# Seven block products for eight in the up projections of four feed-forwards

## The chip, the cores and the metric

The kernel runs on one core of one Trainium2 chip. The metric is the device time of one execution in microseconds (us): 3358.54 us, the median of three runs (3357.44 to 3358.71).

TensorE (PE in the profile) multiplies matrices, VectorE (DVE), ScalarE (ACT) and GpSimd (POOL) do elementwise work, and SyncE (SP) issues the transfers of the weights. PEld is TensorE's loading of the next 128x128 block of weights, beside its matmuls.

## The reference

Two blocks of two layers each, on 512 tokens of width 1024. Block 1 (with 16 meta tokens ahead, 528 in all) has a hybrid mixer and a feed-forward with a convolution. Block 2 has in each layer a feed-forward, then attention (layer 0) or a gated MLP (layer 1), then a second feed-forward. What the change touches is the four feed-forwards of block 2:

```python
def _swiglu_ffn(x, w_gate_up, w_down):
    g, u = jnp.split(x @ w_gate_up, 2, axis=-1)
    return (jax.nn.silu(g) * u) @ w_down

    for i in range(DEPTH):
        x = x + 0.5 * _swiglu_ffn(_rmsnorm(x, ffn1_norm[i]), ffn1_w_gate_up[i], ffn1_w_down[i])
        h = _rmsnorm(x, mix_norm[i])
        ...
        x = x + 0.5 * _swiglu_ffn(_rmsnorm(x, ffn2_norm[i]), ffn2_w_gate_up[i], ffn2_w_down[i])
```

Here x is 512 x 1024, w_gate_up 1024 x 5632 (2816 gates, 2816 values), w_down 2816 x 1024, all in 32-bit floats.

## The kernel before

Features lie on partitions and tokens in columns: h[0..7] are eight tiles of 128 features x 512 tokens (528 in block 1). A product is done in 128x128 blocks of weights ("slabs"). To keep 32-bit precision, weights and operands are each split into a high and a low part of 12 bits, and a slab takes three matmuls: high x high, low operand x high weight, high operand x low weight (`unit`, L204).

The weights come as units of 128 x 1024 (eight slabs, 512 KB). `WStream` (L85) holds all units in the order of their use: SP loads up to three units ahead into `wraw`, ScalarE rounds a half unit (128x512) to the high part `whi` (L124), and VectorE subtracts it from the raw weights to give the low part `wlo` (L125). Four halves of each are held. Every half unit goes through both engines once and is then used by 12 matmuls for each part of the tokens.

In block 2 a matmul has all 512 tokens as columns. In block 1 the 528 tokens (516 in its last up projections) are done in two parts of 264 (258), each with its own weight load.

A feed-forward of block 2 (`ffn2`, L534) has 22 tiles of gates and 22 of values, a unit each. `ffn_seq` (L349) goes through them in three groups, and puts the down products of a group behind the second tile of the next. For each tile VectorE multiplies the two sums by 1/rms (`yg`, `yv`), ScalarE applies silu, VectorE multiplies, and the product is split into `ghi` (ScalarE) and `glo` (VectorE). The down products of a group add into h, a tile of 128 features at a time. When a tile of h is final, `prep` (L273) makes the operands `xhi`, `xlo` of what comes next and adds its squares to `ssq`; `finish_norm` makes 1/rms of it later, beside the first unit, since it scales the result and not the operand.

The tile framework's scheduler sets the order on each engine from the order of the code and its own costs; each engine then works in that order. Sums lie in PSUM: tiles `g` and `s`, four of 512 columns each.

Of the kernel before, what the change touches and what calls it, by code (L numbers as in the profile page):

```python
# [21 lines left out]
# tokens that the last convolution of block 1 reads, in two even parts  # L22
# [7 lines left out]
FGROUPS = ((0, 6), (6, 14), (14, 22))  # L30
LEVELS = (1, 2, 4, 8, 16, 32, 64)
# [7 lines left out]
# w_in column tiles of block 1 in the order they are worked on  # L39
# [45 lines left out]
class WStream:  # L85
    """Weight units in the order of their use: loaded ahead, then split exactly into two parts of 12 bits, by halves."""

    RAW = 3
    SPLIT = 4
    HALF = 4 * P  # L90

    def __init__(self, nc, pool):
        self.nc, self.pool = nc, pool
        self.items, self.halves = [], []
        self.raw, self.sp = {}, {}
        self.n_dma = self.n_split = self.i = 0

    def add(self, key, ap):
        n = ap.shape[1]
        for a in range(0, n, self.HALF):  # L100
            self.halves.append((len(self.items), a, min(n, a + self.HALF)))
        self.items.append((key, ap, len(self.halves)))

    def _dma(self, upto):
        while self.n_dma < min(upto, len(self.items)):
            ap = self.items[self.n_dma][1]
            t = self.pool.tile([P, 2 * self.HALF], F32, tag="raw", name="wraw", bufs=self.RAW)
            n = ap.shape[1]
            for a, b in ((0, n),) if self.n_dma else ((0, self.HALF), (self.HALF, n)):
                self.nc.sync.dma_start(t[:, a:b], ap[:, a:b])  # L110
            self.raw[self.n_dma] = t
            self.n_dma += 1

    def prime(self, n):
        self._dma(n)

    def _split(self, upto):
        while self.n_split < min(upto, len(self.halves)):
            u, a, b = self.halves[self.n_split]
            self._dma(u + self.RAW)  # L120
            t, n = self.raw[u], b - a
            hi = self.pool.tile([P, self.HALF], F32R, tag="hi", name="whi", bufs=self.SPLIT)
            lo = self.pool.tile([P, self.HALF], F32R, tag="lo", name="wlo", bufs=self.SPLIT)
            self.nc.scalar.activation(out=hi[:, 0:n], in_=t[:, a:b], func=AF.Copy)  # L124
            self.nc.vector.tensor_tensor(lo[:, 0:n], t[:, a:b], hi[:, 0:n].bitcast(F32), ALU.subtract)  # L125
            self.sp[self.n_split] = (hi, lo, n // P)
            self.n_split += 1

    def prepare(self, n):
        self._split(n)  # L130

    def get(self, key):
        """the parts (hi, lo, slabs) of the next unit, one after the other"""
        u = self.halves[self.i][0]
        k, _, end = self.items[u]
        assert k == key, (k, key)
        while self.i < end:
            i = self.i
            self.i += 1
            self._split(i + self.SPLIT - 1)  # L140
            yield self.sp.pop(i)


class Model:
    def __init__(self, tc, io):
        assert set(self.MERGE) == set(range(KD))
        self.tc, self.nc, self.io = tc, tc.nc, io
        self.pending_norm = None
        self.later = []
        self.slabwise = False  # L150
        self.budget = 0.0
        self.table, self.table_load, self.table_users = None, None, []

# [18 lines left out]
    def after(self, later, earlier):  # L172
        """issue order on one engine"""
# [4 lines left out]
    def act(self, out, a, f, **k):  # L178
        """activations keep to the order of their tables, so that a table is loaded once for all that use it in a row"""
# [14 lines left out]
    def split_scaled(self, src, gcol, hi, lo):  # L194
        """hi + lo = src * gcol"""
# [8 lines left out]
    def unit(self, key, x, new=None, ps=None, first=True, final=True):  # L204
        """psum of w^T x over the slabs of a unit, in three passes"""
# [3 lines left out]
        k, last = 0, self.ws.items[self.ws.halves[self.ws.i][0]][1].shape[1] // P - 1  # L209
# [26 lines left out]
    def new_g2(self):  # L236
        """a unit of block 1 in two tiles of the other kind, for when they have nothing else to do"""
        return self.new_s(), self.new_s()

    def new_s(self):  # L240
        return self.psum.tile([P, 512], F32, tag="s", name="s", bufs=4)

    def hv(self, k):
        """the tokens that the present block works on"""
# [24 lines left out]

    def xg(self, k):  # L270
# [25 lines left out]
    def means(self, parts, ones, src):  # L296
        """means over partitions, of both parts that src is split into"""
# [1161 lines left out]
```

## Time and profile before

| | |
|---|---|
| median of three runs | 3358.54 us |
| profiled execution, first to last instruction (its span) | 3354.3 us |
| PE busy | 3335.8 us (99%), 19462 matmuls |
| PEld busy | 2894.8 us (86%) |
| DVE busy | 1891.4 us (56%) |
| ACT busy | 1440.1 us (43%) |
| DMA | 298 MB, 89 GB/s on average |

The time of the profiled execution is known only by its span, which is 4.2 us under the median of the runs. The rows of a matmul's busy time overlap each other, so the pace of TensorE is read from how many matmuls a stretch holds, not from how long one takes. The first weights of block 2's four feed-forwards are loaded at 1310, 1953, 2308 and 2961 us; attention lies between the first two feed-forwards, the gated MLP between the last two.

### The profile page before, as it was taken

The page shows a single profiled execution, that of the slowest core. Times are in us where ns is not written, and L with a number is a line of the kernel's source. Part 1 is how long each engine was busy: PE and PEld are TensorE (multiplying, and loading weights), DVE is VectorE, ACT ScalarE, POOL GpSimd, SP SyncE. Part 2 cuts the span into 40 slices and gives each one's busy share as a digit, 9 for nine tenths or more (in the row PEclk, how much of TensorE's full clock was granted, in tenths as well). Part 3 has the DMA queues.
Part 4 walks back from the last instruction along what each step waited for, and adds up shares of the span by engine and source line. Part 5 has one row for each costly group of instructions (what it writes and reads, how often), then busy time and mean ns, then how long its engine had stood idle before and what let it go on. Part 6 is the DMA issues. An engine that isn't in the chain of part 4 may idle for free.

```text
span 3354.3 us, 48141 instructions
## 1 busy us (share of the span) xinstructions
PE 3335.8 (99%) x19462; PEld 2894.8 (86%) x19462; DVE 1891.4 (56%) x3412; ACT 1440.1 (43%) x2531; POOL 15.8 (0%) x41
## 2 busy tenths in 40 slices
PE   8999999999999999999999999999999999999999
PEld 8999999999999998888887778888888888888887
DVE  7766665667665756544446764445444546554443
ACT  5664343456643435332346642324332335343322
POOL 1000000000000000000000000000000000000000
PEclk9999999999999999999999999999999999999999
DMA  3122322322223233233322123333233332223332
GB/s 127 58 64 89 90 93 89 94 76 64 70 89 95 89 95 95 87 102 94 95 88 67 45 85 94 95 95 94 90 100 94 96 118 88 88 89 94 96 96 91
DMA packets 85647, 298.24 MB, mean 89 GB/s; under 512 B 9761, under 2 KB 9761, under 8 KB 85297
## 3 DMA queue, kind: packets, MB, share of 16 engines
q1 hardware_dynamic: 83664, 289.51, 28.0%
q8 instruction: 153, 2.51, 0.3%
q0 software_dynamic: 1328, 3.56, 0.3%
q10 hardware_dynamic: 432, 2.10, 0.2%
q14 instruction: 70, 0.57, 0.1%
HBM read 293.03 MB, written 2.10 MB: 88 GB/s over the span
## 4 chain that ended last, share of the span: by engine, by line
PE 97%; ACT 1%; DVE 1%; DMA 0%; issue 0%; SPq 0%; ACTq 0%
PE g L192 89%; PE s L192 8%; DMA wraw<-w_in 0%; PE s L1182 0%; PE s L1149 0%; ACT L182 0%; DVE am L1169 0%; ACT p L186 0%; PE s L772 0%; PE s L1215 0%; ACT whi L124 0%; DVE wlo L125 0%; PE s L831 0%; ACT rtmp L186 0%; DVE s L161 0%
## 5 line engine op out<-in xcount | busy, mean ns | idle before, releaser
L124 ACT ACTIVATE whi<-wraw 128x512 fp32r<-128x512 f32 x1112 | 691.6, 623 | 1533.8 <-PE g L192 1460.3
L125 DVE TENSOR_TENSOR wlo<-wraw,whi 128x512 fp32r<-128x512 f32 x1112 | 749.2, 675 | 545.6 <-ACT whi L124 523.4
L192 PE MATMUL g<-xhi,whi 128*128 128x512 f32 (+2 forms) x3696 | 1052.6, 332 | 1.0 <-ACT whi L124 1.0
L192 PE MATMUL g<-xlo,whi 128*128 128x512 f32 (+2 forms) x3696 | 1047.1, 331 | 0.0
L192 PE MATMUL g<-xhi,wlo 128*128 128x512 f32 (+2 forms) x3696 | 1046.3, 331 | 0.2 <-DVE wlo L125 0.2
L192 PEld LDWEIGHTS g<-xhi,whi 128*128 128x128 f32 x3696 | 627.0, 189 | 72.6 <-ACT whi L124 1.2
L192 PEld LDWEIGHTS g<-xhi,wlo 128*128 128x128 f32 x3696 | 626.7, 189 | 65.9 <-DVE wlo L125 0.6
L192 PEld LDWEIGHTS g<-xlo,whi 128*128 128x128 f32 x3696 | 624.3, 189 | 66.7
L192 PE MATMUL g<-glo,whi 128*128 128x512 f32 (+1 forms) x1360 | 469.7, 366 | 0.1
L192 PE MATMUL g<-ghi,whi 128*128 128x512 f32 (+1 forms) x1360 | 469.8, 367 | 0.0
L192 PE MATMUL g<-ghi,wlo 128*128 128x512 f32 (+1 forms) x1360 | 469.7, 367 | 0.0
L192 PEld LDWEIGHTS g<-glo,whi 128*128 128x128 f32 x1360 | 244.0, 188 | 45.8 <-DVE glo L161 0.5
L192 PEld LDWEIGHTS g<-ghi,whi 128*128 128x128 f32 x1360 | 244.0, 188 | 45.3 <-ACT ghi L186 0.2
L192 PEld LDWEIGHTS g<-ghi,wlo 128*128 128x128 f32 x1360 | 243.8, 188 | 45.5
L161 DVE TENSOR_TENSOR yv<-g,rstd 128x512 f32<-128x512 f32 x88 | 60.9, 692 | 132.7 <-PE g L192 132.7
L170 DVE SCALAR_TENSOR_TENSOR h<-g,h 128x512 f32<-128x512 f32 x96 | 66.4, 692 | 120.6 <-PE g L192 120.6
L161 DVE TENSOR_TENSOR yg<-g,rstd 128x512 f32<-128x512 f32 x88 | 60.9, 692 | 130.0 <-PE g L192 129.9
L161 DVE TENSOR_TENSOR h<-g,h 128x512 f32<-128x512 f32 (+2 forms) x84 | 58.4, 697 | 92.8 <-PE g L192 92.8
L186 ACT ACTIVATE ghi<-yv 128x512 fp32r<-128x512 f32 x88 | 55.5, 631 | 121.4 <-DVE yv L161 121.4
L192 PE MATMUL g<-whi,xhi 128*128 128x512 f32 x256 | 102.6, 401 | 0.0
L192 PE MATMUL g<-whi,xlo 128*128 128x512 f32 x256 | 101.3, 396 | 0.0
L192 PE MATMUL g<-wlo,xhi 128*128 128x512 f32 x256 | 101.2, 397 | 0.0
(322 smaller groups left out, 3038.5 us busy)
## 6 DMA issues: line engine op xcount, KB each, us to landing
wraw<-w_up SPq DMA_DIRECT2D x88, 512.0 KB, 3.5
wraw<-w2a_up SPq DMA_DIRECT2D x88, 512.0 KB, 3.5
wraw<-w2b_up SPq DMA_DIRECT2D x88, 512.0 KB, 3.5
wraw<-w_in SPq DMA_DIRECT2D x51, 512.0 KB, 3.5
wraw<-w_down SPq DMA_DIRECT2D x32, 512.0 KB, 3.5
wraw<-w2a_down SPq DMA_DIRECT2D x32, 512.0 KB, 3.5
wraw<-w2b_down SPq DMA_DIRECT2D x32, 512.0 KB, 3.5
wraw<-wa_in SPq DMA_DIRECT2D x24, 512.0 KB, 3.5
```

The source lines that it names most:

```text
L124: self.nc.scalar.activation(out=hi[:, 0:n], in_=t[:, a:b], func=AF.Copy)
L125: self.nc.vector.tensor_tensor(lo[:, 0:n], t[:, a:b], hi[:, 0:n].bitcast(F32), ALU.subtract)
L161: self.nc.vector.tensor_tensor(out, a, b, op)
L170: self.nc.vector.scalar_tensor_tensor(out=out, in0=a, scalar=s, in1=b, op0=op0, op1=op1)
L186: i = self.nc.scalar.activation(out=out, in_=a, func=f, **k)
L192: self.nc.tensor.matmul(out, lhsT, rhs, start=start, stop=stop, **k)
```

## The change

The up product of a feed-forward of block 2 is cut into pairs of feature tiles: one pair has two gate tiles and two value tiles (512 columns of w_gate_up), and there are eleven pairs. The operand is cut in two halves of the tokens (256 each) and two halves of the 1024 input features; the weights of a pair in two halves of the input features (11, 12 and 21, 22: feature tile, input half). This 2x2 by 2x2 block product is done as seven products and sums (the form of Strassen's method by Winograd) and not as eight. A product ("step") has 256 columns of tokens, four slabs for the gates and four for the values, so 24 matmuls of 128x256.

- `add_pair`, `_hi`: of seven steps two take the weights as loaded, one takes the loaded block after it served in sums, and the others take sums. VectorE makes four sums of 128x1024 for a pair. Each step's 128x1024 of weights is split into whi (ScalarE) and wlo (VectorE) in one instruction each. Down weights are split in one instruction of 128x768 (512 in the last group).
- `prep_first`, `prep_second`, `prep_pair` take the place of `prep` ahead of these feed-forwards: the operands of the seven steps are sums and differences of the token halves of h[k] and h[k + 4] (slots 0 to 6), so final tiles come in the order 0, 4, 1, 5, 2, 6, 3, 7 (`PAIRED`).
- `ffn2`: three PSUM tiles of two banks, chains a, b, c, take the steps in the order of `STEPS`; four steps add into chain a. ScalarE copies a or c out after steps 0, 1 and 2 (`ev`), VectorE subtracts these copies from later sums. Two PSUM tiles `s` are left for the down products.
- `pair_seq`: the pairs go in groups of 3, 3, 3 and 2; the eight down products of a group stand between the steps of the next group's first pair, those of the last group at the end.
- `open_stage`: inside a feed-forward four more raw tiles and two more whi and wlo tiles of 128x1024 are there, beside three raw and two of each.
- Tiles of block 1, attention and the gated MLP move to shared buffers (`shared`) to make room; the stream of weights may run one half unit further ahead there.

The core of the diff:

```diff
-FGROUPS = ((0, 6), (6, 14), (14, 22))
...
+PGROUPS = ((0, 3), (3, 6), (6, 9), (9, 11))
+PAIRED = (0, 4, 1, 5, 2, 6, 3, 7)
...
+        def step(n):
+            k = key + (n,)
+            if n == 0:
+                self.part(k, get("11", 0), 1024, 0, (), True)
+            elif n == 1:
+                a21, a22 = get("21", 1), get("22", 2)
+                s = get("s", None)
+                self.part(k, s, 1024, 0, ((s, a21, a22), (a21, a21, st["11"])), True)
+            elif n == 2:
+                self.part(k, st["11"], 1024, 0, ((st["11"], st["11"], st["s"]),), True)
+            elif n == 3:
+                self.part(k, get("12", 3), 1024, 0, (), True)
+            elif n == 4:
+                self.part(k, st["21"], 1024, 0, (), True)
+            elif n == 5:
+                self.part(k, st["12"], 1024, 0, ((st["12"], st["12"], st["11"]),), True)
+            else:
+                self.part(k, st["22"], 1024, 0, (), True)
...
+        for o, x, y in sums:
+            self.nc.vector.tensor_tensor(self._tile(o), self._tile(x), self._tile(y), ALU.add)
...
+        self.nc.scalar.activation(out=hi, in_=self._tile(src)[:, a:a + n], func=AF.Copy)
...
+        self.nc.vector.tensor_tensor(lo, self._tile(src)[:, a:a + n], hi.bitcast(F32), ALU.subtract)
...
+    STEPS = ((0, "a", True), (1, "c", True), (4, "a", False), (2, "b", True), (5, "a", False), (3, "c", False),
+             (6, "a", False))
...
+    def prep_first(self, k, g, ng):
+        n = self.T // 2
+        a, b = self.hv(k)[:, 0:n], self.hv(k)[:, n:2 * n]
...
+        self.tt(d, a, b, ALU.subtract)
+        self.act(self.slot(k, 0), a, AF.Copy, scale=ng)
+        self.act(self.slot(k, 1), d, AF.Copy, scale=g)
+        self.stt(self.slot(k, 0, True), a, ng, self.slot(k, 0).bitcast(F32), ALU.mult, ALU.subtract)
+        self.stt(self.slot(k, 1, True), d, g, self.slot(k, 1).bitcast(F32), ALU.mult, ALU.subtract)
+
+    def prep_second(self, k, g1, g2):
...
+        self.act(b2, h2, AF.Copy, scale=g2)
+        self.stt(t[:, 0:n], d, g1, b2[:, n:2 * n], ALU.mult, ALU.add)
+        self.stt(t[:, n:2 * n], b1, g1, b2[:, n:2 * n], ALU.mult, ALU.subtract)
+        self.tt(t4, b2[:, 0:n], t[:, 0:n], ALU.subtract)
+        for v, f in ((lambda lo: self.slots(k, 4, lo), t), (lambda lo: self.slots(k, 2, lo), b2), (lambda lo: self.slot(k, 6, lo), t4)):
+            self.act(v(False), f, AF.Copy)
+        for v, f in ((lambda lo: self.slots(k, 4, lo), t), (lambda lo: self.slots(k, 2, lo), b2), (lambda lo: self.slot(k, 6, lo), t4)):
+            self.tt(v(True), f, v(False).bitcast(F32), ALU.subtract)
...
+    def pair_step(self, key, n, ps):
+        s, _, start = self.STEPS[n]
+        w = self.T // 2
+        for wh, wl, _ in self.ws.get(key + (n,)):
+            for e in range(2):
+                o = ps[:, e, 0:w]
+                for k in range(4):
+                    c = slice((4 * e + k) * P, (4 * e + k + 1) * P)
+                    xh, xl = self.slot(k, s), self.slot(k, s, True)
+                    self.mm(o, wh[:, c], xh, start and k == 0, False, skip_group_check=not start)
+                    self.mm(o, wh[:, c], xl, False, False, skip_group_check=not start)
+                    self.mm(o, wl[:, c], xh, False, k == 3, skip_group_check=not start)
...
+                    if m < 3:
+                        self.act(ev[m], (a, c, a)[m], AF.Copy)
+                    elif m == 3:
+                        self.tt(y[:, :, 0, 0:w], b, ev[0], ALU.subtract)
+                    elif m == 4:
+                        self.tt(y[:, :, 1, w:], a, ev[1], ALU.subtract)
+                        self.tt(y[:, :, 1, w:], y[:, :, 1, w:], each(r[:, w:]), ALU.mult)
+                    elif m == 5:
+                        self.tt(y[:, :, 0, w:], c, ev[2], ALU.subtract)
+                        self.tt(y[:, :, 0, :], y[:, :, 0, :], each(r), ALU.mult)
+                        self.act(y[:, 0, 0, :], y[:, 0, 0, :], AF.Silu)
+                    else:
+                        self.tt(y[:, :, 1, 0:w], a, each(r[:, 0:w]), ALU.mult)
+                        self.act(y[:, 0, 1, :], y[:, 0, 1, :], AF.Silu)
+                        for f in range(2):
+                            self.tt(y[:, 1, f, :], y[:, 0, f, :], y[:, 1, f, :], ALU.mult)
+                            self.split(y[:, 1, f, :], ghi[n % 4][:, f, :], glo[n % 4][:, f, :])
```

TensorE's order in an up product of block 2 (`xhi`, `xlo`: operands; the numbers tell buffers apart). Before, the first slabs of a unit:

```order
L192 MATMUL g<-xhi_78,whi 128x512
L192 MATMUL g<-xlo_86,whi 128x512
L192 MATMUL g<-xhi_78,wlo 128x512
L192 MATMUL g<-xhi_79,whi 128x512
L192 MATMUL g<-xlo_87,whi 128x512
L192 MATMUL g<-xhi_79,wlo 128x512
```

Now, the first slabs of step 0 of a pair (slot 0 of h[0], h[1] and so on lies in every second operand buffer):

```order
L348 MATMUL chaina<-xhi_78,whi_111 128x256
L348 MATMUL chaina<-xlo_86,whi_111 128x256
L348 MATMUL chaina<-xhi_78,wlo_113 128x256
L348 MATMUL chaina<-xhi_80,whi_111 128x256
L348 MATMUL chaina<-xlo_88,whi_111 128x256
L348 MATMUL chaina<-xhi_80,wlo_113 128x256
```

A matmul has half the columns, and 168 of them stand where the same four tiles (two of gates, two of values) had 96.

VectorE's order in the middle of a feed-forward's up product. Before, a gate tile and a value tile (half a pair's work):

```order
L161 TENSOR_TENSOR yg<-g,rstd 128x512
L125 TENSOR_TENSOR wlo<-wraw,whi 128x512 x2
L161 TENSOR_TENSOR yv<-g,rstd 128x512
L125 TENSOR_TENSOR wlo<-wraw,whi 128x512
L161 TENSOR_TENSOR yv<-yg,yv 128x512
L161 TENSOR_TENSOR glo<-yv,ghi 128x512
L125 TENSOR_TENSOR wlo<-wraw,whi 128x512
```

Now, from the middle of a pair on (`wraw<-wraw,wraw` is a sum of weights, `y<-chain,ev` a subtraction of a copy):

```order
L317 TENSOR_TENSOR y_14059<-chainc,ev_14057 128x2x256
L317 TENSOR_TENSOR y_14059<-y_14059,rstd 128x2x512
L259 TENSOR_TENSOR wlo_14067<-wraw_14063,whi_14065 128x1024
L317 TENSOR_TENSOR y_14059<-chainb,rstd 128x2x256
L317 TENSOR_TENSOR y_14059<-y_14059 128x512
L259 TENSOR_TENSOR wlo_114<-wraw_14062,whi_112 128x1024
L317 TENSOR_TENSOR glo_14054<-y_14059,ghi_14050 128x512
L317 TENSOR_TENSOR y_14059<-y_14059 128x512
L243 TENSOR_TENSOR wraw_14062<-wraw_14062,wraw_14063 128x1024
L317 TENSOR_TENSOR glo_14054<-y_14059,ghi_14050 128x512
L259 TENSOR_TENSOR wlo_113<-wraw_14061,whi_111 128x1024
L243 TENSOR_TENSOR wraw_14063<-wraw_108,wraw_109 128x1024
```

The low parts are twice as long, and the sums of weights of the next pair stand between them and the work on the results.

VectorE's order where attention's output projection ends and the second feed-forward begins (h_73 and h_77 are the last two tiles of h). Before:

```order
L161 TENSOR_TENSOR h_77<-g,h_77 128x512
L125 TENSOR_TENSOR wlo<-wraw,whi 128x512 x2
L170 SCALAR_TENSOR_TENSOR xlo_93<-h_77,cols,xhi_85 128x512
L161 TENSOR_TENSOR ssq<-ssq,sq 128x512
L125 TENSOR_TENSOR wlo<-wraw,whi 128x512 x2
L161 TENSOR_TENSOR nsplit<-ssq,nsplit 128x512
```

Now:

```order
L326 SCALAR_TENSOR_TENSOR ops<-h_73,cols,ops 128x256
L317 TENSOR_TENSOR dt<-ops 128x256
L317 TENSOR_TENSOR xlo_93<-ops,xhi_85 128x512
L317 TENSOR_TENSOR tx<-ops,tx 128x512
L317 TENSOR_TENSOR tx<-dt,tx 128x256
L317 TENSOR_TENSOR ssq<-ssq,sq 128x512
L243 TENSOR_TENSOR wraw_19805<-wraw_108,wraw_109 128x1024
L259 TENSOR_TENSOR wlo_114<-wraw_110,whi_112 128x1024
L243 TENSOR_TENSOR wraw_108<-wraw_108,wraw_110 128x1024
L259 TENSOR_TENSOR wlo_19811<-wraw_19805,whi_19809 128x1024
```

The low parts of the feed-forward's first weights (wlo_114 is that of step 0) moved behind all the work on the operands; before, they stood between it.

## Rows read from the trace of the kernel before

**Rows 1.** The page: busy time, and TensorE's share and clock in 40 slices
```profile
PE 3335.8 (99%) x19462; PEld 2894.8 (86%) x19462; DVE 1891.4 (56%) x3412; ACT 1440.1 (43%) x2531; POOL 15.8 (0%) x41
...
PEclk9999999999999999999999999999999999999999
```
**Rows 2.** Windows: stretch, engines' busy us (instructions), clock; 264, 258, 512 columns
```profile
500.00:600.00 100.00, 100.00 (x822) 100.00 (x821) 53.52 (x79) 34.64 (x53) 0.00 (x0) 1.00 0.30 92
970.00:990.00 20.00, 20.00 (x168) 20.00 (x168) 14.57 (x22) 9.89 (x15) 0.00 (x0) 1.00 0.27 81
2100.00:2200.00 100.00, 100.00 (x432) 80.93 (x432) 44.64 (x68) 31.55 (x50) 0.00 (x0) 1.00 0.31 95
```
**Rows 3.** TensorE in order of time, near 1838 us: start, us; six, then four matmuls
```profile
1838.26 0.83 PE L192 MATMUL s<-av,aT 128*128 128x128 f32 x6
1838.92 0.60 PE L1182 MATMUL s<-ident,p 128*128 128x128 f32 x4
1839.36 0.39 PE L192 MATMUL s<-av,aT 128*128 128x128 f32 x2
```
**Rows 4.** VectorE's groups by line and shape: busy us, mean ns of one | idle before
```profile
L125 DVE TENSOR_TENSOR wlo<-wraw,whi 128x512 fp32r<-128x512 f32 x1064 | 729.1, 686 | 545.6 <-ACT whi L124 523.4 <-PE s L192 8.7 <-PE g L192 8.2
L125 DVE TENSOR_TENSOR wlo<-wraw,whi 128x256 fp32r<-128x256 f32 x48 | 20.0, 417 | 0.0
L161 DVE TENSOR_TENSOR yg<-g,rstd 128x512 f32<-128x512 f32 x88 | 60.9, 692 | 130.0 <-PE g L192 129.9
L161 DVE TENSOR_TENSOR glo<-yv,ghi 128x512 fp32r<-128x512 f32 x88 | 60.9, 692 | 58.4 <-ACT ghi L186 58.3
```
**Rows 5.** VectorE in order of time, the end of attention's output projection
```profile
1953.09 0.68 DVE L161 TENSOR_TENSOR h<-g,h 128x512 f32<-128x512 f32 x1
1953.69 0.68 DVE L125 TENSOR_TENSOR wlo<-wraw,whi 128x512 fp32r<-128x512 f32 x1
1954.29 0.68 DVE L161 TENSOR_TENSOR h<-g,h 128x512 f32<-128x512 f32 x1
1954.89 0.74 DVE L170 SCALAR_TENSOR_TENSOR xlo<-h,cols,xhi 128x512 fp32r<-128x512 f32 x1
1955.55 0.68 DVE L161 TENSOR_TENSOR ssq<-ssq,sq 128x512 f32<-128x512 f32 x1
...
1960.10 0.75 DVE L170 SCALAR_TENSOR_TENSOR xlo<-h,cols,xhi 128x512 fp32r<-128x512 f32 x1 [0.20 <-ACT xhi L186]
```
**Rows 6.** ScalarE in order of time, the same place
```profile
1948.13 0.62 ACT L186 ACTIVATE ssq<-h 128x512 f32<-128x512 f32 x1
1948.65 0.71 ACT L186 ACTIVATE xhi<-h,cols 128x512 fp32r<-128x512 f32 x1
1949.27 0.62 ACT L186 ACTIVATE sq<-h 128x512 f32<-128x512 f32 x1
1949.79 0.62 ACT L124 ACTIVATE whi<-wraw 128x512 fp32r<-128x512 f32 x1
```
**Rows 7.** TensorE's waits between 1900 and 2000 us: in total, times, longest
```profile
PE s L1182 <- DVE p L170: 3.0, 1, 3.0
PE g L192 <- DVE wlo L125: 0.7, 1, 0.7
```
**Rows 8.** Windows at the end of attention's heads, columns as in rows 2
```profile
1930.00:1935.00 5.00, 4.39 (x22) 2.71 (x21) 3.15 (x9) 1.92 (x7) 0.00 (x0) 1.00 0.01 2
1935.00:1940.00 5.00, 2.42 (x11) 2.21 (x12) 1.56 (x4) 1.78 (x4) 0.00 (x0) 0.71 0.00 0
1940.00:1945.00 5.00, 4.46 (x24) 3.35 (x23) 2.13 (x7) 1.98 (x7) 0.00 (x0) 0.95 0.00 0
```
**Rows 9.** DMA issues by line: count, KB each, median us to landing
```profile
wraw<-w2a_up SPq DMA_DIRECT2D x88, 512.0 KB, 3.5
```

More of the change, by code (lines that the diff above doesn't have):

```diff
@@ L88 @@
     RAW = 3
-    SPLIT = 4
+    SPLIT = 2
     HALF = 4 * P
     def __init__(self, nc, pool):
[L93 to L98, printed above, removed]
-        n = ap.shape[1]
[L100 to L112, printed above, removed]
@@ L129, in prepare @@
-    def prepare(self, n):
-        self._split(n)
-    def get(self, key):
[L134 to L137, printed above, removed]
+        self.nc = nc
+        self.raws = [pool.tile([P, 1024], F32, name=f"wraw{i}") for i in range(self.RAW)]
+        self.his = [pool.tile([P, 1024], F32R, name=f"whi{i}") for i in range(self.SPLIT)]
+        self.los = [pool.tile([P, 1024], F32R, name=f"wlo{i}") for i in range(self.SPLIT)]
@@ new lines, in __init__, with item, part @@
+        self.items, self.parts = [], []
+        self.slot_of, self.taken = {}, set()
+        self.half_of, self.held = {}, {}
+        self.age = 0
+        self.used_at = {}
+        self.n_load = self.n_hi = self.n_lo = self.i = 0
+        self.stage = None
+    def item(self, ap, stage=None):
+        self.items.append([ap, stage, 0])
+        return len(self.items) - 1
+    def part(self, key, src, n, a=0, sums=(), wide=False):
+        for o, x, y in sums:
+            for t in (o, x, y):
+                self.items[t][2] += 1
+        self.items[src][2] += 2
+        self.parts.append((key, src, a, n, sums, wide))
@@ new lines, in add, with slabs, add_pair, get @@
+    def add(self, key, ap, stage=None, wide=False):
+        n = ap.shape[1]
+        t = self.item(ap, stage)
+        for a in range(0, n, n if wide else self.HALF):
+            self.part(key, t, n if wide else min(n - a, self.HALF), a, (), wide)
+    def slabs(self, key):
+        n, i = 0, self.i
+        while i < len(self.parts) and self.parts[i][0] == key:
+            n += self.parts[i][3] // P
+            i += 1
+        return n
+    def add_pair(self, key, quad, stage):
+        st = {}
+        def get(n, i):
+            if n not in st:
+                st[n] = self.item(quad[i] if i is not None else None, stage)
+            return st[n]
+        def step(n):
[16 more added lines that the diff above has]
+                self.part(k, st["22"], 1024, 0, (), True)
+        return step
@@ new lines, in _oldest, with _load @@
+    def _oldest(self, free):
+        return min(free, key=lambda x: self.used_at.get(x, -1))
+    def _load(self, upto=None):
+        while self.n_load < min(len(self.items), upto or len(self.items)):
+            ap, stage, _ = self.items[self.n_load]
+            own = stage is not None and stage == self.stage
+            if ap is None and not own:
+                return
+            free = [s for s in range(len(self.raws)) if s not in self.taken and (own or s < self.RAW)]
+            if not free:
+                return
+            extra = [s for s in free if s >= self.RAW]
+            s = min(extra or free, key=lambda x: self.used_at.get(("r", x), -1))
+            self.taken.add(s)
+            self.slot_of[self.n_load] = s
+            if ap is not None:
+                n = ap.shape[1]
+                t = self.raws[s][:, 0:n]
+                for a, b in ((0, n),) if self.n_load else ((0, self.HALF), (self.HALF, n)):
+                    self.nc.sync.dma_start(t[:, a:b], ap[:, a:b])
+            self.n_load += 1
@@ new lines, in _lo, with _ahead @@
+    def _lo(self):
+        key, src, a, n, sums, wide = self.parts[self.n_lo]
+        hs = self.half_of[self.n_lo]
+        c = (hs[0] % 2) * self.HALF
+        hi, lo = self.his[hs[0] // 2][:, c:c + n], self.los[hs[0] // 2][:, c:c + n]
+        self.nc.vector.tensor_tensor(lo, self._tile(src)[:, a:a + n], hi.bitcast(F32), ALU.subtract)
+        self._drop(src)
+        self.n_lo += 1
+        self._load()
+    def _ahead(self):
+        while True:
+            more = self._hi()
+            while self.n_lo < self.n_hi and (not self.parts[self.n_lo][5] or self.n_lo < self.n_hi - 1):
+                self._lo()
+                more = True
+            if not more:
+                return
@@ L334, in units @@
                             ws.add((1, l, kind, g, kp), io["wa_in"][2 * n + g, kp])
-                for half, order in enumerate((AOUT_ORDER, range(KD))):
+                for half, order in enumerate((AOUT_ORDER, PAIRED)):
                     for m in order:
@@ L357, in ffn_seq, with pair_seq, pair_units @@
         return seq
+    def pair_seq(self):
+        seq = []
+        for gi, (a, b) in enumerate(PGROUPS):
+            for p in range(a, b):
+                late = list(PAIRED) if gi and p == a else []
+                for n in range(7):
+                    seq.append(("step", p, n))
+                    if n and late:
+                        seq.append(("down", gi - 1, late.pop(0)))
+                seq += [("down", gi - 1, m) for m in late]
+        return seq + [("down", len(PGROUPS) - 1, m) for m in PAIRED]
+    def pair_units(self, key, up, down):
+        step = {}
+        for what, n, m in self.pair_seq():
+            if what == "step":
+                if m == 0:
+                    step[n] = self.ws.add_pair(key + ("pair", n), up[n], key)
+                step[n](m)
+            else:
+                a, b = PGROUPS[n]
+                self.ws.add(key + ("down", n, m), down[m][:, 2 * a * P:2 * b * P], key, wide=True)
     def ffn_units(self, key, up, down):
@@ L431, in block1, with down_order @@
             self.mixer1(l)
[L432 to L434 removed]
             self.ffn1(l)
+    def down_order(self, l, b):
+        return PAIRED if l + 1 == DEPTH and b == KF else range(KD)
     def ffn1(self, l):
```

290 lines of the change are left out of this document (202 added, 88 removed).

## The prediction

> **What bounds the kernel now.** I read the page's busy times and its 40 slices first. TensorE is busy for 3335.8 of 3354.3 us, at the higher clock (2.4 GHz) in nearly every slice, VectorE for 56% [rows 1]. So nothing but TensorE's work sets the end, and the question is what half as many columns in a matmul cost there, and whether the other engines still keep up. The windows answer the first. A stretch in block 2 with nothing but 512-column matmuls holds 432 in 100 us, 231.5 ns each; one in block 1 with 264 columns holds 822, 121.7 ns each; one with 258 columns holds 168 in 20 us, 119.05 ns each, all with TensorE at 100% and the clock at 1.00 [rows 2]. A matmul's price is close to proportional to its columns, although each has its own weight load. For the second question I read VectorE's groups (a 512-wide operation lasts 0.69 us, a 256-wide one 0.42 us [rows 4]) and then its order of time where it is dense: there 512-wide operations start 0.60 us apart, scalar_tensor_tensor ones 0.66 us apart, each before the one in front has ended [rows 5].
>
> **The gain on TensorE.** For a pair of gate and value tiles 4 x 8 x 3 = 96 matmuls of 512 columns go and 7 x 24 = 168 of 256 come. With 11 pairs and four feed-forwards that is 4224 and 7392. The 256 columns are not in the trace; from 264 and 258 the slope is (121.7 - 119.05) / 6 = 0.43 ns a column, so 118.2 ns. Before: 4224 x 0.2315 = 977.9 us. After: 7392 x 0.1182 = 873.7 us. The gain is 104 us (2.4 us a pair). Bounds: with the 258-column price itself it is 98 us, with half of the 512-column price 122 us. I take 104. The down products keep their matmuls (528 for a feed-forward, 122.2 us).
>
> **VectorE and ScalarE beside it.** A 1024-wide operation is not shown; the slope between 256 and 512 is (686 - 417) / 256 = 1.05 ns an element [rows 4], so it lasts 1.22 us, and starts 0.60 + 0.54 = 1.14 us apart in a dense stretch. A pair needs on VectorE seven low parts and four sums of weights (11 x 1.14 = 12.5 us), nine 512-wide operations on results (three subtractions, a scaling of step 4's result, one of step 6's, two products, two low parts: 9 x 0.60 = 5.4 us) and one 1024-wide scaling (1.14 us): 19.1 us. Before it was 16 operations of 0.60 us, 9.6 us. TensorE needs 168 x 0.1182 = 19.86 us for a pair. So in the pairs without down products (8 of 11) VectorE goes from 43% of TensorE's time to 96%: the cover is nearly gone. In the three pairs that carry down products TensorE has 19.86 + 144 x 0.2315 = 53.2 us, and VectorE 19.1 + 8 x (0.87 + 0.66) = 31.3 us, so there it catches up. Its bounds for a bare pair: by start distances 19.1 us, by full durations 11 x 1.22 + 1.22 + 9 x 0.69 = 20.9 us, and with its two waits for ScalarE's high part (58.4 us over 88, 0.66 us each [rows 4]) 22.3 us. The dense stretch is the nearest row, with one idle moment of 0.20 us in it [rows 5], so I take no price but 0.2 us for a pair: 32 x 0.2 = 6 us in all. Its other end is 32 x (22.3 - 19.9) = 78 us.
>
> ScalarE's 512-wide operations start 0.52 us apart [rows 6], so a pair costs it 7 x 1.06 + 7 x 0.52 (three copies, two silus, two high parts) = 11.1 us of 19.86: hidden. SP loads 2 MB a pair as before; a 512 KB load lands in 3.5 us [rows 9] and there are seven raw tiles: hidden, and if not, a sum waits on VectorE with all low parts queued behind it.
>
> **The starts of the four feed-forwards.** Here the cover is missing. For each two tiles of h VectorE now does two additions to h (1.2 us), the operands (256-wide 0.33 us, as scalar_tensor_tensor 0.39: 3 x 0.33 + 4 x 0.39 + 2 x 0.60 = 3.75 us) and two additions of squares (1.2 us): 6.15 us, against 2 x (0.60 + 0.66 + 0.60) = 3.7 us before; low parts of weights come on top.
> - Second feed-forward of layer 0, behind attention: TensorE has 8 x 12 x 0.2315 = 22.2 us of output projection. VectorE begins after the first tile (2.8 us), has 4 x 6.15 + 4 x 0.60 = 27.0 us, and only then, by the order shown, a sum and the low part of step 0 (2.3 us): 32.1 us. TensorE, which needs that low part in its third matmul, stands still for about 10 us. Before, the same place cost it 0.7 us [rows 7].
> - First feed-forward of layer 1: the down products in front are as short (four slabs), the same sum gives 10 us, with two PSUM tiles instead of four.
> - Second of layer 1: eight slabs a tile, 44.5 us for TensorE, 34 us for VectorE, which keeps up. What is left comes behind the last tile: one addition to h, the second half of an operand, three sums and a low part, about 8 us, against step 0 (2.8 us): 6 us, with a wait for ScalarE in it.
> - First of layer 0: eight slabs too, but two sums of squares and two norms; the tail as before (6 us), and eight scalings of h (8 x 0.66) and some eight operations of the second norm (8 x 0.60) fall into pairs where VectorE has no room: 10 us more, 16 us.
> Sum 42 us. The bounds: 15 us, if the first steps overlap all but the missing low part; 63 us, if each of the 32 hand-overs between ScalarE and VectorE (eight a start) adds the 0.66 us seen above.
>
> **The rest.** After 3 us of waiting in attention the granted clock was 0.71 in the next 5 us and 0.95 in the 5 after that, so for a time at the lower level (1.2 GHz): (0.29 + 0.05) x 5 = 1.7 us lost [rows 7, 8]. Four starts: 7 us (0 to 15). At the end of each feed-forward the last pair's results have a chain of five VectorE operations and two of ScalarE (about 4 us), where before the last tile had seven older slabs in front of it (4.9 us); now four slabs of two tiles, 1.4 us each, interleaved: 2 us each, 8 us (0 to 12). Block 1 keeps its arithmetic; its stream of weights may run half a unit further ahead: nothing, by up to 5 us either way.
>
> **The sum.** 104 - 6 - 42 - 7 - 8 = 41 us less. The profiled execution's 3354.3 us would become a span of 3313 us; runs lie 4.2 us above it, so 3358.5 - 41 = 3318 us (rounded). The likeliest case's own range is 3293 to 3345.
>
> **Rivals.**
> A. The stalls at the starts are mostly filled. TensorE's order there already mixes steps, and VectorE may run ahead of what I counted. Then the stalls come to 25 us: 3358.5 - 104 + 25 = 3280 us. For it: VectorE's dense stretch loses only 0.7 us of TensorE's time [rows 7]. Against: the order puts step 0's low part behind all operands. Chance 0.20.
> B. VectorE becomes the bound in the 32 bare pairs. Mechanism: it works strictly in order; a low part waits for ScalarE, and everything behind it too, the subtractions that free chain a among it, so TensorE waits at the next step. Price 22.3 us a pair: 3358.5 - 104 + 57 + 78 = 3390 us, slower by 31 us. It decides from (104 - 57) / 32 = 1.5 us a pair over TensorE's 19.9, so 21.3 us. For it: 96% leaves no room. Against: starts 0.60 us apart though whole operations last 0.69 us [rows 5]. Chance 0.13. [...]
> C. Smaller matmuls don't get cheaper in proportion. Matmuls of 128 columns go at 0.66 us / 6 = 110 ns, not at a quarter of 231.5 [rows 3]. On a straight line from there to 512 columns, 256 would cost 150.5 ns, 7392 of them 1112 us, 134 us more than before: 3358.5 + 134 + 63 = 3556 us. The first are accumulations into the same columns, but the transposes beside them, which add nothing up, go at the same 110 ns [rows 3], and 258 columns go at 119 ns [rows 2]. Chance 0.02. The Trainium skill (TensorE: Matmul & The Clock Gate, "Back-to-back issue gap") gives sustained spacings of 81 ns at 128 columns and 131 ns at 512, by which halving would cost, as an estimate on that page's line, 98 ns and lose time in the same way. The trace disagrees with both figures (110 and 231.5 ns).
>
> **How the numbers follow.** Forecast 0.65, A 0.20, B 0.13, C 0.02. A difference under 0.2% (6.7 us) can't be told from none. Faster: A, all but 0.04 of the forecast's 0.65, and nothing of B and C: 0.81. Within 0.2%: 0.03 of the forecast's and 0.02 of B's tail: 0.05. Slower: 0.14. The range 3275 to 3372 takes in A's centre, the forecast and B's near side, with some 0.2 left outside.
>
> **What would show it.** 7392 matmuls of 256 columns at 118 to 119 ns in windows of a bare pair; VectorE at about 95% there and TensorE at 100%, in pairs of 19.9 to 20.2 us (B if VectorE is at 100% and a pair takes over 21.3). TensorE idle 5 to 16 us at each of the four starts, with wlo or an operand as the releaser, and a dip of the clock behind. Wrong would be: idle spread evenly over the pairs, waits for DMA in the sums, or a price of 256 columns over 125 ns.

## The result: 46.9 us faster, and where it came from

The changed kernel takes 3311.1 us (median of 4 runs, 3304.7 to 3312.6) against 3358.0 us for the kernel before (here with a fourth run): ratio 0.9859, 95% interval 0.9845 to 0.9873. The forecast was 3318 us. The profiled execution took 3310.3 us, its span is 3308.4 us (3354.3 before, [rows 1]).

The page after, with engine, busy time, share of the span and instructions, then the busy tenths of TensorE and VectorE and TensorE's granted clock in 40 slices:

```profile
PE 3249.3 (98%) x22630; PEld 2987.4 (90%) x22630; DVE 2345.7 (71%) x3714; ACT 1610.1 (49%) x2619; POOL 15.8 (0%) x41
PE   8999999999999999999999979999999999999999
DVE  7766665667666657977756788787977756578786
PEclk9999999999999999999999989999999999999999
```

TensorE still sets the end, but no longer at 99%: its slice 24 (attention's end and the start of the second feed-forward) is at 7, and the clock falls there as well. VectorE goes from 56% [rows 1] to 71%, with two slices at 9.

Both traces hold every matmul (22630 and 19462, that is 7392 - 4224 more), so the time of the same matmul can be compared in both. By stage, in us:

| stage | before, us | after, us | difference, us |
|---|---|---|---|
| block 1, up to the first matmul of block 2 | 1330.3 | 1334.5 | +4.2 |
| first feed-forward, layer 0 | 369.0 | 356.4 | -12.6 |
| attention, up to step 0 | 260.8 | 271.2 | +10.5 |
| second, layer 0, up to step 0 of the next | 368.6 | 358.8 | -9.9 |
| first, layer 1 | 368.3 | 348.0 | -20.3 |
| gMLP, up to step 0 | 285.2 | 288.2 | +3.1 |
| second, layer 1, and the end | 372.2 | 351.2 | -21.0 |

The four feed-forwards have the same TensorE work. That they gain between 10 and 21 us, and that attention loses 10, is what is to be explained. These are single executions: stages that an edit below does not touch still differ by up to 4 us from the same stage here (block 1 by -2.3 us in run 1 and by +2.8 in run 2, gMLP by +3.8 in run 4), so a difference of that size in one stage does not show a cause by itself. Windows of the kernel after (stretch, length, busy us and instructions by engine, granted clock):

```profile
1342.90:1347.90 5.00, 5.00 (x24) 5.00 (x25) 5.00 (x5) 1.07 (x2) 0.00 (x0) 0.50 0.37 125
1361.00:1381.00 20.00, 17.37 (x127) 16.40 (x126) 20.00 (x28) 14.05 (x18) 0.00 (x0) 0.91 0.19 53
1462.20:1482.00 19.80, 19.80 (x170) 19.80 (x169) 16.87 (x17) 9.42 (x11) 0.00 (x0) 1.00 0.36 106
1482.00:1501.80 19.80, 19.80 (x170) 19.80 (x169) 19.43 (x22) 10.53 (x14) 0.00 (x0) 1.00 0.32 88
1501.80:1554.80 53.00, 53.00 (x314) 46.86 (x313) 35.80 (x42) 20.36 (x26) 0.00 (x0) 1.00 0.36 107
```

The last three are pairs 4, 5 and 6 of the first feed-forward (counted from 0): the bare ones, 4 and 5, which carry no down products, are 19.81 us from first matmul to first matmul (168 of 117.9 ns), TensorE is never idle, VectorE is at 85% and 98%. The second row lies in pair 1, but for its first 1.7 us: VectorE full, TensorE with 127 matmuls where a bare pair's pace gives 170, at a clock of 0.91. The first is just behind the start: clock 0.50, matmuls 0.213 us apart. Pairs 0, 1 and 2 of the first feed-forward take 28.2, 25.2 and 21.2 us; of the other three pair 0 takes 28.3, 25.9 and 26.8 us, and pairs 1 and 2 19.8 to 20.1.

VectorE's groups answer to [rows 4] (busy us, mean ns of one):

```profile
L259 DVE TENSOR_TENSOR wlo<-wraw,whi 128x512 fp32r<-128x512 f32 x584 | 400.1, 687 | 232.4 <-ACT whi L248 213.7 <-PE g L348 8.2 <-PE s L348 4.4
L259 DVE TENSOR_TENSOR wlo<-wraw,whi 128x1024 fp32r<-128x1024 f32 x308 | 375.5, 1224 | 86.0 <-ACT whi L248 85.8
L243 DVE TENSOR_TENSOR wraw<-wraw,wraw 128x1024 f32<-128x1024 f32 x176 | 215.4, 1224 | 4.1 <-DMA wraw<-w2b_up 1.0 <-DVE wlo L259 0.3
```

A 1024-wide operation lasts 1.22 us, as worked out ahead, and the sums hardly wait for their loads (1.0 us). TensorE's longest waits, in total, number of waits, longest:

```profile
PE chaina L348 <- DVE h L317: 6.4, 1, 6.4
PE s L348 <- ACT whi L248: 6.3, 1, 6.3
PE s L348 <- ACT nsplit L342: 6.2, 6, 4.4
PE s L348 <- DVE wlo L259: 6.0, 2, 5.8
PE s L1503 <- DVE p L326: 4.8, 1, 4.8
```

The second is the kernel's own beginning, the fifth attention's (3.0 before, [rows 7]). The other three are new, each for the most part one single wait at a start: step 0 of the second feed-forward of layer 0 waits for an addition to h that frees its PSUM tile, then its norm; the down products in front of layer 1 wait for their low part. VectorE in order of time at the first of these, about 1960 us:

```profile
1960.08 0.70 DVE L317 TENSOR_TENSOR ssq<-ssq,sq 128x512 f32<-128x512 f32 x1
1960.68 0.70 DVE L317 TENSOR_TENSOR h<-g,h 128x512 f32<-128x512 f32 x1
1961.29 0.69 DVE L317 TENSOR_TENSOR h<-s,h 128x512 f32<-128x512 f32 x1
...
1966.27 0.71 DVE L317 TENSOR_TENSOR ssq<-ssq,sq 128x512 f32<-128x512 f32 x1
1966.87 1.24 DVE L243 TENSOR_TENSOR wraw<-wraw,wraw 128x1024 f32<-128x1024 f32 x1
1968.01 1.24 DVE L259 TENSOR_TENSOR wlo<-wraw,whi 128x1024 fp32r<-128x1024 f32 x1
```

TensorE issued the last matmul of the output projection at 1955.3; the additions of its results are late because operands and squares of earlier tiles stand in front of them, and step 0's low part comes 7 us later still. VectorE has no gap between 1953.6 and 1975.5.

### The profile page after: what moved, and what is told of

Same layout as the page of the kernel before. It is cut to its first block, busy times and chain, and to the rows that moved or that the text cites. A ratio compares the mean times of both kernels' runs of the same rounds, so it can differ in the third digit from the quotient of the medians.

```text
span 3308.4 us, 54928 instructions
## 1 busy us (share of the span) xinstructions
PE 3249.3 (98%) x22630; PEld 2987.4 (90%) x22630; DVE 2345.7 (71%) x3714; ACT 1610.1 (49%) x2619; POOL 15.8 (0%) x41
## 4 chain that ended last, share of the span: by engine, by line
PE 93%; DVE 4%; ACT 2%; DMA 1%; issue 0%; SPq 0%; DVEq 0%; ACTq 0%
PE g L348 45%; PE s L348 22%; PE chaina L348 9%; PE chainb L348 9%; PE chainc L348 7%; DVE wlo L259 1%; DMA wraw<-w_in 0%; DVE h L326 0%; DVE ssq L317 0%; DVE wraw L243 0%; PE s L1503 0%; DMA wT<-g_ws 0%; ACT whi L248 0%; PE s L1470 0%; ACT L338 0%
## 5 line engine op out<-in xcount | busy, mean ns | idle before, releaser
L248 ACT ACTIVATE whi<-wraw 128x512 fp32r<-128x512 f32 (+2 forms) x1004 | 781.4, 780 | 1350.3 <-PE g L348 649.4
L259 DVE TENSOR_TENSOR wlo<-wraw,whi 128x512 fp32r<-128x512 f32 (+2 forms) x1004 | 873.5, 873 | 319.7 <-ACT whi L248 300.6
L348 PE MATMUL g<-xhi,whi 128*128 128x264 f32 (+2 forms) x2288 | 500.7, 295 | 1.7 <-ACT whi L248 1.7
L348 PE MATMUL g<-xhi,wlo 128*128 128x264 f32 (+2 forms) x2288 | 494.3, 292 | 0.2 <-DVE wlo L259 0.2
L348 PE MATMUL g<-xlo,whi 128*128 128x264 f32 (+2 forms) x2288 | 492.2, 292 | 0.0
L348 PEld LDWEIGHTS g<-xhi,whi 128*128 128x128 f32 x2288 | 362.7, 190 | 9.2 <-ACT whi L248 1.9
L348 PEld LDWEIGHTS g<-xhi,wlo 128*128 128x128 f32 x2288 | 362.3, 190 | 5.9 <-DVE wlo L259 0.4
L348 PE MATMUL s<-ghi,wlo 128*128 128x512 f32 x704 | 277.0, 394 | 5.8 <-DVE wlo L259 5.8
L348 PE MATMUL s<-ghi,whi 128*128 128x512 f32 x704 | 278.3, 396 | 2.8 <-DVE h L326 1.6
L348 PE MATMUL s<-glo,whi 128*128 128x512 f32 x704 | 276.9, 394 | 0.0
```

The costliest lines, as they stand in the source:

```text
L248: self.nc.scalar.activation(out=hi, in_=self._tile(src)[:, a:a + n], func=AF.Copy)
L259: self.nc.vector.tensor_tensor(lo, self._tile(src)[:, a:a + n], hi.bitcast(F32), ALU.subtract)
L348: self.nc.tensor.matmul(out, lhsT, rhs, start=start, stop=stop, **k)
```

## The experiments

Times are medians; the kernel before gave 3357.4 to 3358.7 us beside them, and 3311.1 us of the changed kernel is what "less" and "more" refer to.

**1. Three of the four sums left out.**
```diff
-            self.nc.vector.tensor_tensor(self._tile(o), self._tile(x), self._tile(y), ALU.add)
+            if self.items[o][0] is None:
+                self.nc.vector.tensor_tensor(self._tile(o), self._tile(x), self._tile(y), ALU.add)
```


> Leaves out three of the four sums of weights of every pair (the raw tile is split as it is), so VectorE has 3 x 1.14 = 3.4 us less in a pair; nothing else changes. If VectorE's queue is what TensorE waits for at the starts and only there: bare pairs of the middle stay at 19.81 us, pairs 0 to 2 of the first feed-forward (74.6 us now, 59.4 without loss) lose some 10 us of their excess, the other three starts 3 to 4 us each, 3290 us or so (15 to 25 less than the changed kernel). If TensorE waits for ScalarE's high parts or pays for its clock instead: under 5 us less.

3296.7 us, 14.4 less (ratio to before 0.9816, 0.9801 to 0.9831), just short of the 15 to 25 expected. Bare pairs of the middle stay at 19.81 us although VectorE falls to 64% and 83% there. Pairs 0 to 2 of the first feed-forward lose 7.8 us, of the last two 3.1 and 2.5; at the second, behind attention, nothing (68.2 and 68.4 us), where 3 to 4 were expected. So the sums cost TensorE time only where VectorE has a backlog, and behind attention the backlog is not made of them.

**2. The sums on GpSimd.** The same line with `self.nc.gpsimd`.

> The four sums of weights of a pair go from VectorE to GpSimd, which is idle there; same arithmetic. No row shows a sum of 1024 columns on GpSimd. Up to 19.8 / 4 = 4.9 us for one it stays below TensorE's pair, and the starts gain as with the sums left out or a little more (15 to 30 us less than the changed kernel, 3280 to 3296 us). Above 4.9 us for one GpSimd is the bound of the 28 bare pairs: at 6 us a pair would take 24 us, 3430 us or so. A rival: while GpSimd works VectorE's own operations get longer than 1.22 and 0.69 us, and bare pairs go over 19.81 us though GpSimd is not full.

3368.5 us, 57 more (ratio 1.0031, 1.0020 to 1.0043: slower than the kernel before). One sum takes GpSimd 2.79 us, four of them 11.1 us where a bare pair has 19.8, so GpSimd is not full. But VectorE's own operations stretch. GpSimd's group first (busy us, mean ns), then in order of time (start, length) three of GpSimd's sums on end and three of VectorE's low parts beside them:

```profile
L243 POOL TENSOR_TENSOR wraw<-wraw,wraw 128x1024 f32<-128x1024 f32 x176 | 490.6, 2788 | 2037.4 <-DVE wlo L259 661.4 <-DMA wraw<-w2b_up 644.3 <-PE g L348 539.1
```
```profile
1573.97 9.10 POOL L243 TENSOR_TENSOR wraw<-wraw,wraw 128x1024 f32<-128x1024 f32 x3 [9.65 <-DVE wlo L259]
...
1575.58 1.89 DVE L259 TENSOR_TENSOR wlo<-wraw,whi 128x1024 fp32r<-128x1024 f32 x1 [1.75 <-ACT whi L248]
1578.43 2.38 DVE L259 TENSOR_TENSOR wlo<-wraw,whi 128x1024 fp32r<-128x1024 f32 x1 [0.96 <-ACT whi L248]
1581.19 2.97 DVE L259 TENSOR_TENSOR wlo<-wraw,whi 128x1024 fp32r<-128x1024 f32 x1 [0.38 <-ACT whi L248]
```

The low part that lasts 1.22 us alone lasts up to 2.97 us here, and up to 3.49 us in the whole run. Not every operation of VectorE stretches. Its groups in this run, each holding operations beside GpSimd's sums and others:

```profile
L259 DVE TENSOR_TENSOR wlo<-wraw,whi 128x1024 fp32r<-128x1024 f32 x308 | 463.3, 1512 | 93.5 <-ACT whi L248 93.5
L317 DVE TENSOR_TENSOR glo<-y,ghi 128x512 fp32r<-128x512 f32 x110 | 117.7, 1082 | 14.7 <-ACT ghi L342 12.5
L317 DVE TENSOR_TENSOR y<-chaina,ev 128x512 f32<-128x512 f32 x44 | 30.1, 685 | 16.6 <-PE chaina L348 16.6
```

The first two read both inputs from SBUF; the mean of the first goes from 1.22 to 1.51 us, that of the second from 0.69 to 1.08. The third reads one input from PSUM and keeps its 0.69 us: the 40 subtractions of this kind (from chains a, b and c) that overlap a sum in time take 0.68 to 0.69 us. So it is not VectorE as a whole that is slowed, but its operations with two inputs in SBUF. Pairs 5 and 8 go to 21.3 us with VectorE "busy" at 100%, pairs 0 to 2 together to between 75.9 and 86.9 us. The rival of this run holds for pairs 5 and 8. In pair 0 VectorE is busy only 81% (first feed-forward) and 89% (second), so there the length of the sums themselves, three of which follow one from another, can count as well; no run separates the two. The Trainium skill (SBUF — State Buffer, "SBUF: two separate sides") says that a VectorE operation with two SBUF inputs and a GpSimd operation that reads SBUF share a port pair as an exclusive lock, which whichever starts first holds for its whole instruction. These rows agree with it: 1.08 and 1.51 us on the mean with two SBUF inputs, 0.69 us with one.

**3. Squares and scalings on GpSimd.**
```diff
-            self.tt(self.ssq[:, 0:T], self.ssq[:, 0:T], sq[:, 0:T], ALU.add)
+            eng = self.nc.gpsimd if self.block == 2 else self.nc.vector
+            eng.tensor_tensor(self.ssq[:, 0:T], self.ssq[:, 0:T], sq[:, 0:T], ALU.add)
...
+                self.nc.gpsimd.tensor_tensor(hm, hm, r1, ALU.mult)
+                self.act(hm, hm, AF.Copy, scale=self.col("final_norm_g", k))
```


> At the starts of the four feed-forwards (and of the two mixers) the additions of squares go to GpSimd (7 of 0.60 us a start, 14 at the first feed-forward), and the eight scalings of h to GpSimd and ScalarE (8 x 0.66 us). VectorE has 4.2 us less at three starts, 13.7 us less at the first. If VectorE's queue sets the stalls, the starts get shorter by about as much: 10 us at the first, 3 to 4 at the others, 3285 to 3297 us in all. If PSUM or ScalarE sets them: no change, within 5 us of the changed kernel.

3327.6 us, 16 more: a miss. One addition takes 1.75 us there (0.69 on VectorE), and they form a chain, so the norm is late. ScalarE's, then TensorE's waits between 1945 and 1990 us:

```profile
ACT nsplit L342 <- POOL ssq L538: 7.3, 1, 7.3
...
PE chaina L348 <- DVE h L317: 9.2, 1, 9.2
PE s L348 <- ACT nsplit L342: 8.0, 1, 8.0
```

The addition to h is late by 9.2 us instead of 6.4, with less work in VectorE's queue: six operations ahead of it, between 1953 and 1973 us, take 1.06 to 1.52 us where the same ones take 0.42 to 0.70 in the changed kernel. This run can't tell whether the backlog is the cause; runs 6, 8 and 9 bear on that.

**4. Four low parts twice in every bare pair.**
```diff
+        again = len(key) == 6 and key[3] == "pair" and key[4] not in (0, 3, 6, 9) and key[5] in (0, 2, 4, 6)
+        for _ in range(2 if again else 1):
```


> In the 28 bare pairs four of the seven low parts of weights are computed twice (the same value into the same tile), 4 x 1.14 = 4.6 us more VectorE work in a pair. If VectorE's price is its start distances (18.1 to 19.1 us a pair now) a bare pair takes 22.7 to 23.7 us with VectorE at 100%, 28 x 3.4 = 95 us more than the changed kernel (70 to 110; the first pairs, already full, pay all of it). If the cover were gone already (every operation added costs its full time): 28 x 4.6 = 128 us more. If VectorE had more room than its busy share says: under 50 us more.

3336.6 us, 25 more instead of 70 to 110: of the three readings only the last (under 50) holds. Windows of pairs 4, 5 and 6:

```profile
1469.90:1489.70 19.80, 19.80 (x170) 19.80 (x169) 18.94 (x19) 8.88 (x10) 0.00 (x0) 1.00 0.25 80
1489.70:1509.50 19.80, 19.80 (x171) 19.80 (x169) 19.80 (x23) 10.65 (x14) 0.00 (x0) 1.00 0.30 94
1509.50:1562.50 53.00, 53.00 (x314) 46.86 (x313) 41.60 (x47) 20.04 (x26) 0.00 (x0) 1.00 0.38 115
```

The bare pairs still take 19.81 us. Of 9.1 us added in pairs 4 and 5, 2.4 us appear there and 5.8 us in pair 6, whose down products give VectorE room (41.6 us busy instead of 35.8); the rest lies ahead of them, where VectorE is at 80% in pair 3 instead of 73%. Of the pairs only 1 and 2, which stand behind a start's backlog, got clearly longer: by 8.5 us in the first feed-forward, by 4.4 to 5.7 in the others. (Another 3.8 us of this execution lie in gMLP, which the edit leaves alone.)

**5. The norm behind step 1.** A dependence holds the norm's two products behind step 1's last matmul in TensorE's order.

> One thing: in TensorE's order the two norm products of a feed-forward's start stand behind the last matmul of step 1, not among the first of step 0, where the trace of the changed kernel shows TensorE standing 4.85 us for them at the second feed-forward and 0.5 to 0.8 at the others. VectorE's work is the same. If TensorE's order costs this time by itself, 4 to 8 us less than the changed kernel (with some of the clock). If VectorE's queue sets the pace up to the end of pair 2, what is gained at the norm is lost at the next low part: within 2 us of the changed kernel.

3311.0 us, the same. TensorE's waits between 1935 and 1985 us:

```profile
PE chaina L348 <- DVE h L317: 6.5, 1, 6.5
PE chainc L348 <- ACT whi L248: 5.9, 1, 5.9
```

The wait of 4.4 us for the norm is gone; one of 5.9 us for the next part of the weights stands in its place. TensorE's order at this place costs nothing by itself.

**6. Late squares.**
```diff
-        self.prep_sq(m)
+        self.squares.append(lambda: self.prep_sq(m))
...
+        for _ in range(4 if n < 2 and self.squares else 0):
+            self.squares.pop(0)()
```


> At the four starts the squares of h (ScalarE) and their additions (VectorE, 7 x 0.60 us, at the first feed-forward 14) come behind steps 0 and 1 of pair 0 instead of ahead of the first low parts; the norm's products follow them. No work is removed. If the place of the work in VectorE's queue sets the stalls, each start gets 4 us shorter, the first up to 8: 12 to 20 us less than the changed kernel, 3291 to 3299 us. If VectorE's total work up to pair 2 sets them, moving gives nothing: within 4 us.

3304.2 us, 6.9 less (ratio 0.9843, 0.9830 to 0.9857; between the two expectations, and the interval overlaps the changed kernel's 0.9845 to 0.9873). In the trace attention's end and the second feed-forward gain 11.1 us, 8.4 of them in the second feed-forward, ahead of layer 1; the first of layer 1 gives 4.0 back. Behind attention the wait for h falls from 6.4 to 3.8 us, and one of 3.2 us for step 0's low part appears. Moving work seems to give something; most of the backlog stays.

**7. As 6, with the norm held and each addition to h ahead of the operands of the tile in front.**

> As with the late squares, and the norm held behind step 1, and each addition to h issued ahead of the operands of the tile in front of it, so that PSUM tiles come free earlier (the first matmul of the second feed-forward waits 6.4 us for the last addition to h). If order is all, 3 to 6 us less than with the late squares alone, most of it at the second feed-forward: 3286 to 3295 us. If the operands' total sets it: the same as the late squares.

3305.0 us, as late squares alone: step 0 behind attention starts 0.7 us earlier, and pair 0 there takes 1.1 us longer.

**8. Operands of steps 4 to 6 left out.** Slots 4 to 6 read the quarters 0 to 2 of the operands; the sums and splits for them are not made.

> Leaves out the operands of steps 4, 5 and 6 of the order (the sums of two quarters of h and their low parts): these steps read the quarters of steps 0 to 3 instead. VectorE has 4 x (2 x 0.40 + 2 x 0.33 + 0.60) = 8.2 us less a start, ScalarE 4 x 0.9 us. TensorE's work is the same. If VectorE's queue sets the stalls, 6 to 8 us less at each start, 25 to 33 us less than the changed kernel, 3278 to 3286 us. If clock and PSUM set them: under 10 us less.

3288.7 us, 22 less (ratio 0.9797, 0.9784 to 0.9810): short of the 25 to 33 expected, far from under 10. TensorE's waits between 1930 and 1980 us:

```profile
PE chaina L348 <- DVE h L317: 1.9, 1, 1.9
...
PE s L348 <- ACT nsplit L342: 0.7, 1, 0.7
```

Behind attention the wait of 6.4 us for h falls to 1.9 us and pair 0 from 28.3 to 23.2 us: 9.6 us, for 8.2 us of VectorE. The wait of the down products in front of layer 1 goes altogether. At the starts with eight slabs in front it is 3.2 us less (first of layer 0) and 1.4 (second of layer 1), no more than stages differ between executions. So the operands are the backlog where TensorE has only four slabs a tile to cover them. (The run takes ScalarE's part of these operands away too, 3.6 us a start; run 9 leaves both as they are.)

**9. More cover instead of less work.**
```diff
-PGROUPS = ((0, 3), (3, 6), (6, 9), (9, 11))
+PGROUPS = ((0, 2), (2, 5), (5, 8), (8, 11))
```


> The 11 pairs' down products in groups of 2, 3, 3, 3 instead of 3, 3, 3, 2: the last group's eight tiles have six slabs each, 8 x 18 x 0.2315 = 33.3 us of TensorE beside the next stage's operands instead of 22.2 us. All work is the same. If the start behind a feed-forward (layer 1, first) costs 12 to 14 us because TensorE has too little work beside VectorE's 27 to 34 us, it falls to 2 to 4 us; the down products of the first group lie in pair 2 then, where VectorE is full now, and take 1 to 4 us off the first feed-forward: 3294 to 3301 us, 10 to 17 less than the changed kernel. If PSUM tiles or the clock set that start: within 4 us of the changed kernel.

3293.6 us, 17.5 less (ratio 0.9808, 0.9795 to 0.9821), the upper end of the 10 to 17 expected. TensorE's waits at the start of layer 1, of the changed kernel (2296 to 2335 us) and of this one (2285 to 2325):

```profile
PE s L348 <- DVE wlo L259: 5.8, 1, 5.8
PE chainb L348 <- ACT whi L248: 1.3, 1, 1.3
PE chainc L348 <- ACT whi L248: 0.8, 1, 0.8
PE s L348 <- DVE h L326: 0.7, 1, 0.7
```
```profile
PE chainb L348 <- ACT whi L248: 1.3, 1, 1.3
PE chainc L348 <- ACT whi L248: 0.8, 1, 0.8
PE chainc L348 <- DVE wlo L259: 0.6, 1, 0.6
PE s L348 <- ACT nsplit L342: 0.5, 1, 0.5
```

The same VectorE work, beside 33.3 instead of 22.2 us of TensorE's, holds nothing up ahead of step 0. Of the 15.6 us that the span lost, 9.8 lie there; the rest is spread over the other stages, 0.1 to 1.9 us in each.

**10. Groups, late squares, and the scalings of h from pair 2 on.** The two diffs above, and the scalings taken in the order of the down products, `elif self.later and key[-1] >= 2`.

> The same groups, with the late squares, and the eight scalings of h at the first feed-forward one by one from pair 2 on, each ahead of its tile's down product, instead of in pairs 0 and 1. If the three are independent: 10 to 17 + 7 + 3 to 6 us less than the changed kernel, 3281 to 3291 us. If the groups already take up VectorE's backlog: no better than the groups alone.

3287.1 us (3286.0 to 3290.4), 24.0 less than the changed kernel and 70.6 less than the kernel before (ratio 0.9791, 0.9777 to 0.9804): the fastest that computes everything. Pairs 0 and 1 of the first feed-forward go from 28.2 and 25.2 to 27.9 and 20.8 us. What is left of the starts is pair 0 everywhere, 26.5 to 27.9 us.

## Why the prediction was right, term by term

- **The gain, 104 us.** Measured 977.9 - 7392 x 0.1179 = 106.3 us, 26.6 a feed-forward. The price is close to proportional to the columns, and rival C is out.
- **Bare pairs, 6 us.** Measured nothing. The count of 19.1 us a pair was near (VectorE 16.9 and 19.4 us in two of them), but the step "the cover is nearly gone" judged each pair by itself. Run 4 shows that it isn't so: the work added in pairs 4 and 5 comes out in pair 6, beside its down products. That it is the seven raw tiles and four split ones that let VectorE lead or lag by several us is a reading of the kernel; no run had fewer of them. Rival B's point of decision, 21.3 us a pair, is wrong for the same reason: with four more operations (4.6 us on top of some 18) nothing happened in the middle. In the changed kernel B exists only in pairs 1 and 2 of the first feed-forward, 6.7 us.
- **The starts, 42 us, the clock, 7 us, and the feed-forwards' ends, 8 us.** Together 57; measured 49.2: what the four feed-forwards gained less than 26.6 us each (14.0, 16.7, 6.3 and 5.6), and 6.6 us that attention's end waited longer for step 0. By start, with the 2.5 + 5.9 us that lie ahead of layer 1 put there, that is 14.0 (first of layer 0), 14.9, 14.7 and 5.6, where 16, 10, 10 and 6 stood without clock and ends. Rival A's 25 us is out. Runs 8 and 9 show the mechanism where TensorE has four slabs a tile in front: VectorE's operands against TensorE's last slabs. At the fourth start TensorE's waits come to 2.4 us, below the 5 to 16 that the prediction named as its sign; the rest of the 5.6 is mostly clock. What was mis-sized is the split. The ends are 5 us: in the first down products, which take the last pair's results, matmuls start later than 0.2315 us behind the one in front by 1.2, 1.8, 1.9 and 0.3 us in all. The clock is 12 us: the stretches at 0.50 near the starts add up to 41 us, TensorE stood for some 14 of them, and the other 27, with a matmul in 0.213 us instead of 0.118, lose 0.45 each. So the stalls themselves are some 32 us, not 42.
- **Its releasers.** "The order puts step 0's low part behind all operands" was right, but the low part is the longest wait at one start only. What TensorE meets first is whatever stands behind the operands: an addition to h that frees PSUM, the norm, ScalarE's high part. Run 5 shows it for two of them: the wait for the norm goes, and one for the high part takes its place.
- **Block 1, nothing; attention and gMLP were not in the sum.** Missed: +4.2, +3.9 (10.5 less the 6.6 above) and +3.1, 11 us. Block 1 loses 2.7 us in its first 49 us; gMLP loses 3.4 us by its 50th matmul, where TensorE waits 3.0 us for VectorE and VectorE 6.5 us for one load (4.8 before). Attention loses 1.4 us at its beginning and the rest around the end of its heads. These were read from one trace each, and none was tried by itself. Part of block 1's loss is lasting (1332.2 to 1337.3 us in the eleven traces with the new code, 1330.3 before); the cause of all three stays open.
- **Sum.** -106.3 + 49.2 + 11.2 = -45.9, the difference of the spans; it closes by construction, since each term is what its stages left over. Against the forecast's 41 us the errors nearly cancel: 2 us too little gain, 6 and 8 us too much loss, 11 us not foreseen. The mechanism was right; that the total came within 5 us is in part luck.

## What to carry to other kernels

When a change trades TensorE work for VectorE work, do not ask only whether the share fits in a steady stage: in run 4 a surplus was carried into the next stage with room. Ask where the new work comes in a burst, what TensorE has left to do beside it, and lengthen that (here by a different grouping of the same products) before moving work to another engine. A wait's releaser names what was last in the queue, not what made the queue long.

## What was not expected of the hardware

- GpSimd and VectorE stand in each other's way: low parts of 1.22 us took up to 3.49 us beside GpSimd sums of 2.79 us, while operations that read one input from PSUM kept their 0.69 us (run 2).
- At the upper level a matmul's pace did not follow the granted clock. In run 8 a hundred us of block 1 had a granted clock of 0.95, with as many matmuls as at 1.00 in the kernel after; the bare pairs 4 and 5 of the first feed-forward, also at 0.95 there, took 19.80 and 19.77 us. Windows, of the kernel after and of run 8:

```profile
1000.00:1100.00 100.00, 100.00 (x698) 93.69 (x697) 61.16 (x94) 38.63 (x62) 0.00 (x0) 1.00 0.31 96
```
```profile
1000.00:1100.00 100.00, 100.00 (x698) 93.69 (x697) 61.26 (x93) 38.54 (x62) 0.00 (x0) 0.95 0.32 96
```

At the lower level it did: 256 columns in 0.213 us are 256 cycles of 1.2 GHz, while 0.118 us are more than 256 cycles of 2.4 GHz (0.107). What sets the 0.118 us is not shown.
